# Convolution taps as three half-length filters, placed by the dense products; one norm chain for four query tiles

## The chip, the cores and the metric

The kernel runs on one core of a Trainium2 chip. The metric is device microseconds (us) of one execution, the median of three runs. The engines are named as in the profile: PE is TensorE's matmul row (PEld its weight loads), DVE is VectorE, ACT is ScalarE, POOL is GpSimd, SP is SyncE, which here issues the DMAs. Each engine works off its own instructions strictly in the order in which they were written down for it; engines meet only at semaphores.

## The reference

Two layers of an encoder trunk over 1024 positions of width 1024, all in float32. The change touches two things inside a layer: the convolution branch and the norms of the attention's queries.

```
h = rms_norm(x); z = h @ w_in[l]                     # 20 column tiles of 128
attention: q (4 tiles), k, v -> QK-norm, 2-D rotary embedding, softmax(q k^T / 8) v
hgrn2: 4 heads, forward and backward gated recurrence (two kernel passes of 2 heads)
conv: u = a * sigmoid(gate)                          # 256 channels, 1024 positions
      y[t] = sum over 31 taps of w[tap] * u[t + tap - 15]
      o_cv = silu(layer_norm(y + b))                 # mean and variance over the channels
x = x + concat(attention, hgrn2, conv) @ w_out[l]
x = x + relu(rms_norm(x) @ w1)^2 @ w2
```

## The kernel before

**Layout.** Everything is held transposed: 128 channels on the partitions, the 1024 positions along the free axis. The 256 convolution channels are two tiles (i = 0, 1). A *dense product* is one column tile of z: eight steps over the contraction (`dense_steps`, line 214), each of six 128x512 matmuls (a float32 product from high and low parts), 48 matmuls into one of two PSUM tiles named S (a ring of two). `evac` (line 321) lets DVE multiply the finished product by the row norm `Rb` into SBUF, and so frees the PSUM tile.

**Order of a layer's first part.** The column tiles come in the order of `ZORDER`: the four of the convolution (`conv_in`), then five of the first recurrence pass, `Hgrn(0).__init__` (lines 408 to 450: column 6 hq, 10 and 12 the two gates, 14 the output gate, 8 the values iv). The values are transposed on PE at the end of the constructor (line 447) and copied by ACT to `vt`. Then `h0.core()` (line 515) runs its steps interleaved with `qkv()` (columns 5 v, 4 k, 0 to 3 q) and with the convolution `cg = conv_all()`: the loop of lines 707 to 709 takes one step of `qg`, `cg`, `qg`, `cg` for each step of the core. After that come the five columns of `Hgrn(1)` (7, 11, 13, 15, 9), with the convolution's tail (`conv_tail`: mean, variance, normalization, silu) taken along in three steps, and then the attention.

**Convolution.** `conv(i)` (line 345) does on DVE one `tensor_scalar` for the middle tap and 30 `scalar_tensor_tensor` (line 357), each over nearly 1024 positions and each adding to the same y. `conv_tail` (line 371) needs both y: POOL adds them, PE sums over the channels (line 162, `tok_sums`, 128x1 results), ACT widens the sums (`widen`, line 168), PE transposes them back (`flip`, line 178), DVE subtracts; then squares, sums, `rstd` and flips again for the variance.

**Recurrence core.** For s = 1, 2, 4 ... 64 line 530 multiplies four slices of X by T, two on POOL and two on DVE, and then DVE's line 531 updates T. From s = 2 on, `scores` copies slices (ACT, line 487), multiplies them on PE (line 499) into banks of the ring e or c (two banks each), and DVE merges them into A (lines 506 and 510). Line 588 makes the output o.

**Norms of q and k.** PE sums squares (line 162); `rstd` (line 147) is a chain of 11 tiny DVE instructions. For k the result is widened and flipped (line 665 multiplies it in); for each of the four q tiles it runs on 16 columns and goes to `nqc`, which the attention's score pass (line 761) reads.

**What sets the order.** A scheduler writes down the order on each engine: it goes through the program in the order in which it is written, with a machine model of its own, and lets an engine take a later instruction when the next one isn't ready in that model. So the order on an engine is fixed before the run, and it needn't suit the real durations.

## Time and profile before

| | |
|---|---|
| median of three runs | 2541.44 us (2540.55 to 2541.88) |
| the profiled execution | 2538.31 us, its span 2536.5 us |
| PE busy | 2457.5 us (97%) |
| DVE busy | 1998.2 us (79%) |
| ACT, POOL busy | 1206.2 us, 734.1 us |
| granted clock of TensorE, mean over the span | 0.984 |

The profile is one execution. Its page gives the busy time of each engine, the chain of work that ended last, and groups of instructions by source line; the trace behind it is asked for stretches of time (windows), instructions in order (timeline), and waits. A granted clock of 1.00 is 2.4 GHz, of 0.50 it is 1.2 GHz. In the text *stretch A* is the time from the end of column 8's product to the recurrence's output o of the first pass (112 to 246 us in layer 0, 1374 to 1506 us in layer 1), *stretch B* the time from there to the start of column 9's product (246 to 302 us, 1506 to 1562 us).

### The profile page before, as it was taken

The numbers are of one execution on the slowest core, as the hardware profiler recorded it, in microseconds if no ns is written. First come the engines' busy times: TensorE is split into PE (matmuls) and PEld (weight loads), VectorE is DVE, ScalarE is ACT, GpSimd is POOL, SyncE is SP. The second block draws the span as 40 slices with busy tenths as digits, with TensorE's granted clock in tenths as the row PEclk, the third lists the DMA queues.
The fourth block names the chain that finished last, engine by engine and source line by source line (L and its number), as shares of the span: only waits on it lengthen the run. The fifth ranks groups of instructions, "written<-read, shape, count | busy, mean of one in ns | idle before, by whom it ended". The sixth has DMA issues, their size and how long they took to land.

```text
span 2536.5 us, 34033 instructions
## 1 busy us (share of the span) xinstructions
PE 2457.5 (97%) x12608; PEld 2024.9 (80%) x12608; DVE 1998.2 (79%) x3051; ACT 1206.2 (48%) x1960; POOL 734.1 (29%) x463
## 2 busy tenths in 40 slices
PE   8989999999999999999999999999999999999999
PEld 7767778878788887888887777888787888878887
DVE  6998599872887778987859985898638877789886
ACT  4222478863544443443433225787635444444332
POOL 0233566533034430000123325664330344200000
PEclk9998999999999999999999999999999999999999
DMA  4101310032244448554131113000322534574442
GB/s 160 57 25 63 104 34 18 14 116 105 75 170 163 141 159 322 160 174 156 67 108 51 42 63 104 17 18 26 133 89 87 173 137 163 187 279 158 161 152 91
DMA packets 113077, 286.99 MB, mean 113 GB/s; under 512 B 11408, under 2 KB 11664, under 8 KB 112912
## 3 DMA queue, kind: packets, MB, share of 16 engines
q1 hardware_dynamic: 112912, 284.83, 32.4%
q8 instruction: 99, 1.62, 0.3%
q14 instruction: 66, 0.54, 0.1%
HBM read 197.75 MB, written 87.03 MB: 112 GB/s over the span
## 4 chain that ended last, share of the span: by engine, by line
PE 79%; DVE 15%; ACT 3%; issue 2%; POOL 1%; DMA 1%; SPq 0%; DVEq 0%; ACTq 0%; POOLq 0%
PE S L223 15%; PE S L1201 10%; PE c L1000 10%; PE S L1000 7%; PE e L1000 7%; PE e L1201 6%; PE c L1201 6%; DVE x L357 4%; PE e L808 4%; PE c L787 4%; PE S L750 3%; PE e L499 2%; PE e L162 1%; PE e L588 1%; DVE wlo L200 1%
## 5 line engine op out<-in xcount | busy, mean ns | idle before, releaser
L223 PE MATMUL S<-xs,whi 128*128 128x512 f32 x1280 | 365.0, 407 | 8.8 <-ACT whi L199 7.4
L223 PEld LDWEIGHTS S<-xs,whi 128*128 128x128 f32 x1280 | 244.2, 194 | 65.0 <-ACT whi L199 7.4
L1201 PE MATMUL S<-xs,xs 128*128 128x512 f32 x816 | 201.6, 390 | 2.6 <-DVE xs L902 2.6
L223 PE MATMUL S<-xs,wlo 128*128 128x512 f32 x640 | 203.4, 399 | 0.0
L901 ACT ACTIVATE xs<-m 128x512 fp32r<-128x512 f32 x216 | 126.0, 619 | 141.6 <-DVE m L912 50.8
L766 POOL TENSOR_SCALAR P<-P,mx 128x1024 f32<-128x1024 f32 x124 | 142.4, 1148 | 164.2 <-DVE mx L765 129.8
L792 DVE TENSOR_TENSOR PT<-c,PT 128x512 fp32r<-128x512 f32 x256 | 171.2, 685 | 23.1 <-ACT PT L791 21.2
L1201 PEld LDWEIGHTS S<-xs,xs 128*128 128x128 f32 x816 | 152.9, 188 | 35.4 <-DVE xs L902 3.5
L791 ACT ACTIVATE PT<-c 128x512 fp32r<-128x512 f32 x256 | 147.7, 593 | 69.9 <-PE c L787 66.3
L199 ACT ACTIVATE whi<-raw 128x1024 fp32r<-128x1024 f32 x56 | 59.1, 1058 | 243.3 <-PE S L223 224.2
L808 PE MATMUL e<-PT,x 128*128 128x256 f32 x1024 | 173.8, 300 | 0.8 <-ACT PT L791 0.5
L761 DVE TENSOR_SCALAR_CACHE_REDUCE P<-S,nqc 128x1024 f32<-128x1024 f32 x124 | 158.6, 1279 | 15.7 <-PE S L750 8.0
L357 DVE SCALAR_TENSOR_TENSOR x<-x,par,x 128x1009 f32<-128x1009 f32 (+14 forms) x120 | 166.9, 1391 | 1.8
L787 PE MATMUL c<-cons,P 128*128 128x128 f32 x992 | 152.8, 278 | 10.5 <-POOL P L766 5.6
L902 DVE TENSOR_TENSOR xs<-m,xs 128x512 fp32r<-128x512 f32 x216 | 145.0, 695 | 22.0 <-ACT xs L901 22.0
L750 PE MATMUL S<-x,QS 128*128 128x512 f32 x480 | 153.9, 419 | 6.0 <-DVE P L761 5.7
L261 POOL TENSOR_TENSOR tmp<-tmp,tmp 128x1024 f32<-128x1024 f32 x19 | 50.6, 2664 | 360.1 <-ACT tmp L260 359.9
L764 ACT ACTIVATE P<-P,mx 128x1024 f32<-128x1024 f32 x124 | 142.5, 1149 | 25.3 <-DVE P L761 24.0
L808 PEld LDWEIGHTS e<-PT,x 128*128 128x128 f32 x1024 | 140.4, 195 | 8.4 <-ACT PT L791 2.0
L787 PEld LDWEIGHTS c<-cons,P 128*128 128x128 f32 x992 | 115.7, 141 | 36.4 <-issue 10.2
L223 PEld LDWEIGHTS S<-xs,wlo 128*128 128x128 f32 x640 | 123.3, 193 | 26.8 <-issue 0.3
L1201 PE MATMUL e<-xs,xs 128*128 128x512 f32 x552 | 140.8, 390 | 0.9 <-ACT xs L901 0.5
(310 smaller groups left out, 5639.0 us busy)
## 6 DMA issues: line engine op xcount, KB each, us to landing
m<-ad SPq DMA_DIRECT2D x104, 512.0 KB, 3.9
ad<-x SPq DMA_DIRECT2D x176, 256.0 KB, 2.2
raw<-w_in_t SPq DMA_DIRECT2D x40, 512.0 KB, 3.3
xs<-w_t SPq DMA_DIRECT2D x36, 512.0 KB, 3.9
raw<-w_t SPq DMA_DIRECT2D x36, 512.0 KB, 3.6
m<-w_t SPq DMA_DIRECT2D x32, 512.0 KB, 6.8
ad<-tmp SPq DMA_DIRECT2D x48, 256.0 KB, 2.3
x<-w_t SPq DMA_DIRECT2D x24, 512.0 KB, 4.8
```

The source lines that it names most:

```text
L223: nc.tensor.matmul(zp[h] if type(zp) is list else zp[:, h, :], w, xx[:, h * 512 : (h + 1) * 512], start=first, stop=last)
L357: nc.vector.scalar_tensor_tensor(y[:, lo:hi], u[:, lo + d : hi + d], par[:, l, wof + tap : wof + tap + 1], y[:, lo:hi], op0=ALU.mult, op1= ...
L750: nc.tensor.matmul(S[:, hb, :], qs, kk[:, hb * 512 : (hb + 1) * 512], start=first, stop=not first)
L761: nc.vector.tensor_scalar(Pt, S, nqc[:, j, ci : ci + 1], 3.0e38, op0=ALU.mult, op1=ALU.min, accum_out=mx[:, 1:2])
L764: nc.scalar.activation(Pt, Pt, AF.Exp, bias=mx[:, 1:2], scale=-1.0, accum_out=mx[:, 2:3])
L787: nc.tensor.transpose(t[:, q * P : (q + 1) * P], Pt[:, hb, q * P : (q + 1) * P], ident)
L791: nc.scalar.activation(hi, src, AF.Copy)
L792: nc.vector.tensor_tensor(lo, src, hi.bitcast(F32), op=ALU.subtract)
L808: nc.tensor.matmul(pvp[:, cs], VS[g][:, hb * 4 + kb, :], pt[:, kb, :], start=hb == 0 and n == 0, stop=hb == 1 and n == 7,)
L902: ordered("v", nc.vector.tensor_tensor(lo, src, hi.bitcast(F32), op=ALU.subtract))
L1000: nc.tensor.matmul(bank, w[i][:, kt * P : (kt + 1) * P], BC[name][kt][j], start=n == 0 and name not in ("M6", "M7", "M3"), stop=n == 11, s ...
L1201: nc.tensor.matmul(banks[dt], w[i][:, dt * P : (dt + 1) * P], a[j], start=n == 0 and name not in ("M6", "M7", "M3"), stop=n == 3 * SG - 1, ...
```

## The change

**Three half-length filters.** u is now written by POOL with its even positions in the first half of the tile and its odd ones in the second (a strided access). With E and O for even and odd taps, the even outputs are E(ue) + O(uo), and the odd ones are (E+O)(ue+uo) - E(ue) - O(uo), suitably shifted. So a convolution tile takes three filters over 512 positions: 15 taps on the even half, 16 on the odd half, 16 on the sum, with an extra column and a small edge correction; then three combining instructions, two of which write y interleaved. In place of 1 + 30 long instructions there are 3 + 44 half-length ones, one sum, three combinations and five tiny ones.

**Where the taps stand.** `behind` ties each `scalar_tensor_tensor` of a filter to the last matmul that `dense` has written down, for the scheduler's order alone: no semaphore comes of it. The constructors now take convolution steps along with their products (`pace`: after which of the eight contraction steps), from the first column on; the loop over `h0.core()` takes fewer. Two steps of the generator are written as one `cg` step. The loop that finished both convolutions before the attention's keys is gone.

**The tail has two more stages**: a stop after each widening.

**Moved.** The transposes of iv go from the constructor into the core (`turned`, after its first step). v's second part is done after contraction step 6 of column 4, not 2.

**Query norms.** Each q tile writes its mean square into `nqc`; one `rstd` chain over 64 columns for all four follows after `qkv` (`query_norms`).

```diff
-    def rstd(src, n, scale):
+    def rstd(src, n, scale, work=None):
...
+    def behind(i):
+        tc.add_manual_dep(i.ins, pe_last[0].ins.name, mybir.DependencyInfo(
+            mybir.DependencyClass.NoSync, mybir.DependencyReason.DATA), reason="order")
...
-        def ztile(col):
+        def ztile(col, pace=()):
             got = []
-            drain(zsteps(col, got.append))
+            for k, _ in enumerate(zsteps(col, got.append)):
+                for _ in range(pace.count(k)):
+                    next(cg, None)
             return got[0]
...
+        def fir(dst, src, taps, shift=0):
+            n, m = dst.shape[1], src.shape[1]
+            for k, (d, w) in enumerate(sorted(taps, key=lambda t: abs(t[0] + shift))):
+                d += shift
+                lo, hi = max(0, -d), min(n, m - d)
+                if k == 0:
+                    nc.vector.tensor_scalar(dst, src[:, d : d + n], w, 0.0, op0=ALU.mult, op1=ALU.add)
+                else:
+                    behind(nc.vector.scalar_tensor_tensor(
+                        dst[:, lo:hi], src[:, lo + d : hi + d], w, dst[:, lo:hi], op0=ALU.mult, op1=ALU.add
+                    ))
+                yield
+
+        def conv_steps(i):
...
+            nc.vector.tensor_tensor(s[:, 1:H], uo[:, 0 : H - 1], ue[:, 1:H], op=ALU.add)
+            yield
+            second = fir(even, ue, [(d, tap(2 * d)) for d in range(-7, 8)])
+            for _ in fir(odd, uo, [(d, tap(2 * d + 1)) for d in range(-8, 8)]):
+                yield
+                if next(second, 1) is None:
+                    yield
+            yield from fir(uo, s, [(d, hs[:, d + 8 : d + 9]) for d in range(-8, 8)], 1)
...
         def conv(i):
-            u = us[i]
...
+            for k, _ in enumerate(conv_steps(i)):
+                if k % 2:
+                    yield
...
-                evac(ztile(8 + ls), iv)
+                evac(ztile(8 + ls, (1, 4) if ls else ()), iv)
+
+            def turned(self):
...
+                self.turned()
...
+        def query_norms():
+            y = rstd(nqc.rearrange("p a b -> p (a b)"), 64, 1.0 / 64, tmp())
...
-                    if k == 2 and rest:
+                    if rest and k == (6 if col == 4 else 2):
...
-        for _ in h0.core():
-            for g in (qg, cg, qg, cg):
-                next(g, None)
+        for n, _ in enumerate(h0.core()):
+            next(qg, None)
+            if n > 3 and n % 4 < 3:
+                next(cg, None)
+            next(qg, None)
         drain(qg)
-        while not ys[1:]:
-            next(cg)
+        query_norms()
```

**Place 1: DVE around the evacuation of column 8 (iv), layer 0.** Before, L327 is `evac`, L357 a tap, L200 the low part of a weight tile; S2_122 is column 8's product.

```order
L327 TENSOR_TENSOR tmp_112_651<-S2_116_658,Rb_76_307 128x1024
L200 TENSOR_TENSOR wlo_121_717<-raw_119_714,whi_120_716 128x1024
L357 SCALAR_TENSOR_TENSOR x8_135_807<-x8_79_341,par_13_76,x8_135_807 128x1017
...
L357 SCALAR_TENSOR_TENSOR x8_135_807<-x8_79_341,par_13_76,x8_135_807 128x1012
L327 TENSOR_TENSOR m4_118_713<-S2_122_720,Rb_76_307 128x1024
L458 TENSOR_TENSOR m4_130_791<-X_93_465 128x512 x2
```

In the changed kernel the same work has the lines L338 (`evac`), L367 (a half-length tap) and L203, and S2_126 is column 8's product:

```order
L367 SCALAR_TENSOR_TENSOR x8_79_341<-x8_102_489,nwa_103_490,x8_79_341 128x511
L367 SCALAR_TENSOR_TENSOR x8_79_341<-x8_102_489,nwa_103_490,x8_79_341 128x509
L338 TENSOR_TENSOR tmp_116_691<-S2_120_698,Rb_76_307 128x1024
L203 TENSOR_TENSOR wlo_125_765<-raw_123_762,whi_124_764 128x1024
L338 TENSOR_TENSOR m4_122_761<-S2_126_768,Rb_76_307 128x1024
L511 TENSOR_TENSOR m4_132_827<-X_93_465 128x512 x2
```

Six taps that stood between the weight tile and the evacuation of iv are gone from there; four half-length ones stand ahead of the evacuation of column 14 (S2_120).

**Place 2: PE at the transposes of iv, layer 0.** Before (S2_134 is the next product, column 5; L447 the transposes):

```order
L223 MATMUL S2_122_720<-xs_50_145,wlo_109_591 128x512 x2
L223 MATMUL S2_134_800<-xs_33_103,whi_114_654 128x512 x2
L223 MATMUL S2_134_800<-xs_34_104,whi_114_654 128x512 x2
L223 MATMUL S2_134_800<-xs_33_103,wlo_115_655 128x512 x2
L223 MATMUL S2_134_800<-xs_35_108,whi_114_654 128x512
L447 MATMUL e_123_770<-cons_14_77,m4_118_713 128x128 x4
```

and now (S2_136 is column 5, L500 the transposes):

```order
L232 MATMUL S2_126_768<-xs_50_145,wlo_113_621 128x512 x2
L232 MATMUL S2_136_836<-xs_33_103,whi_118_694 128x512 x2
L232 MATMUL S2_136_836<-xs_34_104,whi_118_694 128x512 x2
L232 MATMUL S2_136_836<-xs_33_103,wlo_119_695 128x512 x2
L232 MATMUL S2_136_836<-xs_35_108,whi_118_694 128x512 x2
L232 MATMUL S2_136_836<-xs_36_109,whi_118_694 128x512 x2
L232 MATMUL S2_136_836<-xs_35_108,wlo_119_695 128x512 x2
L500 MATMUL e_137_849<-cons_14_77,m4_122_761 128x128 x4
```

Twelve matmuls of column 5 now stand ahead of the transposes, where there were seven.

**Place 3: PE between the convolution's variance sums and the flips of its result, layer 0** (layer 1 has the same order). Before (L162 the sums, L178 the flips, S2_310 column 15's product; the rows left out are 12 more matmuls of it, 19 in all):

```order
L162 MATMUL e_296_2026<-cons_14_77,tmp_289_1959 128x1 x8
L223 MATMUL S2_310_2089<-xs_33_103,whi_281_1878 128x512 x2
L223 MATMUL S2_310_2089<-xs_34_104,whi_281_1878 128x512 x2
L223 MATMUL S2_310_2089<-xs_33_103,wlo_282_1879 128x512 x2
...
L223 MATMUL S2_310_2089<-xs_42_124,whi_281_1878 128x512
L178 MATMUL e_301_2051<-cons_14_77,tmp_300_2049 128x128 x4
L178 MATMUL e_302_2058<-cons_14_77,tmp_300_2049 128x128 x4
```

and now (L165 the sums, L181 the flips, L809 the attention's first two score products, S2_288 column 15 and S2_310 column 9):

```order
L232 MATMUL S2_288_2033<-xs_50_145,wlo_272_1875 128x512 x2
L809 MATMUL S2_300_2134<-x8_259_1795,x8_257_1787 128x512
L165 MATMUL e_293_2095<-cons_14_77,tmp_291_2066 128x1 x8
L809 MATMUL S2_300_2134<-x8_259_1795,x8_257_1787 128x512
L809 MATMUL S2_300_2134<-x8_260_1796,x8_257_1787 128x512 x2
L181 MATMUL e_311_2176<-cons_14_77,tmp_297_2118 128x128 x3
L809 MATMUL S2_303_2145<-x8_259_1795,x8_257_1787 128x512 x2
L809 MATMUL S2_303_2145<-x8_260_1796,x8_257_1787 128x512 x2
L181 MATMUL e_311_2176<-cons_14_77,tmp_297_2118 128x128
L181 MATMUL e_312_2183<-cons_14_77,tmp_297_2118 128x128 x4
L232 MATMUL S2_310_2163<-xs_33_103,whi_276_1949 128x512 x2
```

Three score matmuls now stand between the sums and the flips, where there were 19 of a dense product, and column 9's product starts behind the flips.

**How many.** By the same orders, DVE has between the evacuation of iv and o (stretch A) 31 long taps, one long first tap and 50 tiny norm instructions before, and now 33 half-length taps, two half-length first taps, four half-length sums and combinations and 14 tiny norm instructions. Ahead of it there were 27 long taps, now 34 half-length ones and three first taps; behind it there were two long taps and one q tile's norm chain, now 21 half-length taps, one first tap, three combinations and the chain over 64 columns. Layer 1 has one long tap less in A before and the same now. On ACT, the table for the sigmoid of the convolution's tail is now loaded between the second and the third exponential of the attention, and the one for the exponential again behind it; before, the tail's sigmoids stood ahead of the first exponential.

## Rows read from the trace of the kernel before

**Rows 1.** Windows of the whole core: stretch, its length, busy time of PE, PEld, DVE, ACT and POOL with the number of instructions, granted clock, DMA share and GB/s. The rows are, for layer 0 and then for layer 1, the products ahead of stretch A, stretch A and stretch B.

```profile
59.00:112.00 53.00, 53.00 (x235) 43.92 (x234) 51.00 (x39) 14.86 (x15) 11.35 (x4) 1.00 0.21 73
112.00:246.00 134.00, 119.02 (x759) 93.48 (x758) 125.87 (x188) 35.55 (x51) 44.61 (x20) 0.91 0.13 45
246.00:302.00 56.00, 53.91 (x272) 44.68 (x271) 36.38 (x66) 22.79 (x23) 21.50 (x9) 0.97 0.22 75
...
1374.00:1506.00 132.00, 119.84 (x764) 94.14 (x762) 126.29 (x187) 35.39 (x51) 42.39 (x20) 0.92 0.13 46
1506.00:1562.00 56.00, 53.92 (x269) 44.62 (x269) 34.44 (x66) 23.23 (x23) 22.17 (x9) 0.97 0.23 77
```

**Rows 2.** The chain of work that ended last, inside 112 to 250 us: shares by engine and line.

```profile
by line: PE S L223 14.7%; DVE x L357 14.7%; issue 9.5%; DVE A L510 6.7%; DVE X L530 6.7%; PE e L162 5.4%; PE e L588 5.2%; DVE wlo L200 5.0%; DVE T L531 4.4%; POOL X L530 3.3%; DVE tmp L629 3.2%; PE e L499 3.1%; DVE nwt L154 2.0%; DVE A L506
```

**Rows 3.** Timeline of PE: start, us, line, operation, tiles, count, and in brackets PE's idle time ahead of it and who ended it. Layer 0's waits in stretch A, one of stretch B, then layer 1's two largest.

```profile
116.92 1.97 PE L447 MATMUL e<-cons,m 128*128 128x128 f32 x8 [4.25 <-DVE m L327]
145.50 1.97 PE L642 MATMUL e<-cons,tmp 128*128 128x128 f32 x8 [5.70 <-DVE A L506]
179.66 1.10 PE L178 MATMUL e<-cons,tmp 128*128 128x128 f32 x8 [1.20 <-ACT tmp L168]
189.64 2.67 PE L499 MATMUL e<-m,m 64*128 64x128 f32 x16 [2.02 <-DVE tmp L665]
...
219.61 1.15 PE L544 MATMUL c<-cons,X 128*128 128x128 f32 x8 [1.46 <-ACT T L545]
...
265.66 1.09 PE L178 MATMUL e<-cons,tmp 128*128 128x128 f32 x8 [1.67 <-ACT tmp L168]
...
1379.03 1.97 PE L447 MATMUL e<-cons,m 128*128 128x128 f32 x8 [4.26 <-DVE m L327]
1405.09 1.97 PE L642 MATMUL e<-cons,tmp 128*128 128x128 f32 x8 [2.77 <-DVE A L506]
```

**Rows 4.** Windows of 5 us, columns as in rows 1: behind PE's wait for iv, behind the wait of 2.02 us, and behind the wait of 1.67 us in stretch B.

```profile
115.00:120.00 5.00, 3.08 (x12) 2.79 (x13) 5.00 (x5) 1.19 (x2) 2.45 (x2) 0.50 0.02 3
...
190.00:195.00 5.00, 5.00 (x23) 4.20 (x22) 5.00 (x7) 2.65 (x5) 3.50 (x2) 0.50 0.55 189
...
265.00:270.00 5.00, 4.34 (x23) 3.74 (x24) 2.51 (x3) 1.67 (x2) 0.00 (x0) 1.00 0.36 126
```

**Rows 5.** Timeline of DVE, columns as in rows 3: seven taps in a row, the six ahead of iv's evacuation, that evacuation, a pair of 128x512 merges, a tap beside POOL's rotary product, and from stretch B the steps of the variance's chain (first and last) and the products with the flips.

```profile
69.88 9.14 DVE L357 SCALAR_TENSOR_TENSOR x<-x,par,x 128x1012 f32<-128x1012 f32 x7
105.15 10.58 DVE L357 SCALAR_TENSOR_TENSOR x<-x,par,x 128x1017 f32<-128x1017 f32 x6
115.65 1.22 DVE L327 TENSOR_TENSOR m<-S,Rb 128x1024 f32<-128x1024 f32 x1
...
152.39 1.35 DVE L510 COPY_PREDICATED A<-masks,c 128x512 f32<-128x512 uint8 x2
...
167.88 0.17 DVE L152 TENSOR_SCALAR nwy<-nwa 128x16 int32<-128x16 int32 x1
168.00 1.28 DVE L357 SCALAR_TENSOR_TENSOR x<-x,par,x 128x1016 f32<-128x1016 f32 x1
169.19 0.17 DVE L154 SCALAR_TENSOR_TENSOR nwt<-nwy 128x16 f32<-128x16 f32 x1
...
183.21 3.45 DVE L357 SCALAR_TENSOR_TENSOR x<-x,par,x 128x1023 f32<-128x1023 f32 x1
...
287.36 0.17 DVE L151 TENSOR_SCALAR nwa<-e 128x8 f32<-128x8 f32 x1 [0.45 <-PE e L162]
...
290.42 0.17 DVE L156 SCALAR_TENSOR_TENSOR nwy<-nwt,nwy 128x8 f32<-128x8 f32 x1
292.49 2.48 DVE L399 TENSOR_TENSOR x<-x,e 128x512 f32<-128x512 f32 x4 [1.91 <-PE e L178]
```

**Rows 6.** DVE's groups by line with shapes kept apart, over the whole span: names, shapes, count, busy time in us, mean ns, idle time ahead of them.

```profile
L1013 DVE SCALAR_TENSOR_TENSOR tmp<-tmp,Rb 128x512 f32<-128x512 f32 x64 | 54.1, 866 | 1.3 <-ACT Rb L237 0.9
...
L1013 DVE SCALAR_TENSOR_TENSOR x<-x,Rb 128x512 f32<-128x512 f32 x64 | 42.5, 685 | 0.1
...
L349 DVE TENSOR_SCALAR x<-x,par 128x1024 f32<-128x1024 f32 x4 | 5.3, 1328 | 0.0
```

**Rows 7.** DVE's groups in stretch A of layer 0, columns as in rows 6.

```profile
L357 DVE SCALAR_TENSOR_TENSOR x<-x,par,x 128x1014 f32<-128x1014 f32 (+14 forms) x34 | 45.5, 1340 | 0.2
```

**Rows 8.** Timeline of POOL, columns as in rows 3: the product that makes u, the recurrence's products for s = 4 behind DVE's T, and the rotary product beside the tap of rows 5.

```profile
47.28 2.40 POOL L342 TENSOR_TENSOR x<-tmp,tmp 128x1024 f32<-128x1024 f32 x1 [46.84 <-ACT tmp L340]
...
133.93 4.61 POOL L530 TENSOR_TENSOR X<-X,T 128x512 f32<-128x512 f32 x2 [1.14 <-DVE T L531]
...
181.11 4.47 POOL L627 TENSOR_TENSOR tmp<-tmp,x 128x1024 f32<-128x1024 f32 x1 [16.98 <-DVE tmp L626]
```

**Rows 9.** Timeline of PE in stretch B: the variance sums, the next four matmuls of column 15, and the flips.

```profile
285.49 1.84 PE L162 MATMUL e<-cons,tmp 128*128 128x1 f32 x16
287.19 1.19 PE L223 MATMUL S<-xs,whi 128*128 128x512 f32 x4
...
291.73 1.09 PE L178 MATMUL e<-cons,tmp 128*128 128x128 f32 x8
```

**Rows 10.** Timeline of ACT there: the widening of the variance's result, and the table load ahead of the first exponential.

```profile
290.62 1.06 ACT L168 ACTIVATE tmp<-nwy 128x1024 f32<-128x1024 f32 x1 [1.66 <-DVE nwy L156]
...
301.96 1.28 ACT L436 ACT_TABLE_LOAD   x1
```

More of the change, by code (lines that the diff above doesn't have):

```diff
@@ L145, in lower_bounds @@
         nc.vector.tensor_scalar(oml, lbt, -1.0, 1.0, op0=ALU.mult, op1=ALU.add)
-    def rstd(src, n, scale):
-        a = cst.t([P, 16], "nwa", bufs=2)[:, :n]
-        y = cst.t([P, 16], "nwy", bufs=3)[:, :n]
-        t = cst.t([P, 16], "nwt", bufs=2)[:, :n]
+    def rstd(src, n, scale, work=None):
+        if work is None:
+            a = cst.t([P, 16], "nwa", bufs=2)[:, :n]
+            y = cst.t([P, 16], "nwy", bufs=3)[:, :n]
+            t = cst.t([P, 16], "nwt", bufs=2)[:, :n]
+        else:
+            a, y, t = (work[:, i * n : (i + 1) * n] for i in range(3))
         nc.vector.tensor_scalar(a, src, scale, EPS, op0=ALU.mult, op1=ALU.add)
@@ L341, in conv_in @@
             u = x8()
-            nc.gpsimd.tensor_tensor(u, a, s, op=ALU.mult)
+            nc.gpsimd.tensor_tensor(
+                u.rearrange("p (h n) -> p n h", h=2), a.rearrange("p (n h) -> p n h", h=2),
+                s.rearrange("p (n h) -> p n h", h=2), op=ALU.mult,
+            )
             us.append(u)
-        def conv(i):
-            u = us[i]
-            y = x8()
-            wof = PAR["cw"][0] + i * CK
-            nc.vector.tensor_scalar(
-                y, u, par[:, l, wof + CPAD : wof + CPAD + 1], pv(l, "cb", i), op0=ALU.mult, op1=ALU.add
-            )
-            for tap in range(CK):
-                d = tap - CPAD
-                if d == 0:
-                    continue
-                lo, hi = max(0, -d), min(L, L - d)
-                nc.vector.scalar_tensor_tensor(
-                    y[:, lo:hi], u[:, lo + d : hi + d], par[:, l, wof + tap : wof + tap + 1], y[:, lo:hi],
-                    op0=ALU.mult, op1=ALU.add,
-                )
-                yield
-            ys.append(y)
+        def fir(dst, src, taps, shift=0):
[5 more added lines that the diff above has]
+                    nc.vector.tensor_scalar(dst, src[:, d : d + n], w, 0.0, op0=ALU.mult, op1=ALU.add)
+                else:
+                    behind(nc.vector.scalar_tensor_tensor(
+                        dst[:, lo:hi], src[:, lo + d : hi + d], w, dst[:, lo:hi], op0=ALU.mult, op1=ALU.add
+                    ))
+                yield
@@ L429, in __init__ @@
                 gl = tmp()
-                evac(ztile(14 + ls), gl)
-                if ls == 1:
-                    next(cg, None)
+                evac(ztile(14 + ls, (2, 6) if ls else full[:4]), gl)
                 gate = tmp()
@@ L690, in qpart @@
             nc.sync.dma_start(qd[j], qz)
+        def query_norms():
+            y = rstd(nqc.rearrange("p a b -> p (a b)"), 64, 1.0 / 64, tmp())
+            for j in range(4):
+                nc.vector.scalar_tensor_tensor(
+                    nqc[:, j].rearrange("p (a b) -> p a b", b=2),
+                    y[:, 16 * j : 16 * j + 16].rearrange("p (a b) -> p a b", b=2), -0.125,
+                    rc.unsqueeze(2).to_broadcast([P, 8, 2]), op0=ALU.mult, op1=ALU.mult,
+                )
         def qkv():
```

56 lines of the change are left out of this document (41 added, 15 removed).

## The prediction

> **What bounds the kernel now.** I read the windows first [rows 1], then the chain inside the one that stands out [rows 2], then PE's and DVE's timelines there. Ahead of stretch A PE is busy 53.0 of 53.0 us, so nothing that DVE saves there can be won. In stretch A of layer 0 PE works 119.0 of 134.0 us and DVE 125.9, and the clock row is 0.91. PE's loss is therefore 15.0 us of idle time and, at the lower of its two levels (1.2 GHz) for part of the time, about 0.09 x 134 x (119/134) = 10.7 us of slow work: 25.7 us together. In layer 1 it is 132.0 - 119.8 = 12.2 and 0.08 x 132 x 0.91 = 9.6, 21.8 us. DVE idles only 8.1 and 5.7 us there. In stretch B the picture is turned round: PE 53.9 of 56.0, DVE 36.4. So stretch A is paced by both engines, with DVE the fuller one; B is paced by PE.
>
> The chain agrees [rows 2]: DVE's taps (L357) hold 14.7% of it, as much as the dense products (L223), beside the recurrence's steps on DVE and POOL (L510, L530, L531) and 9.5% of issue. The waits are the visible part [rows 3]: PE stands 4.25 us for iv, because iv's evacuation starts at 115.65 behind six taps that took 10.58 us [rows 5]; 5.70 us (layer 1: 2.77) for a merge into A; and 1.20, 2.02 and 1.46 us elsewhere. Behind a wait the clock may be down: 0.50, that is 1.2 GHz, in the 5 us behind the waits of 4.25 and 2.02, but 1.00 behind that of 1.67 [rows 4].
>
> **The taps' price.** Seven long taps take 9.14 us, 1.31 each [rows 5]; the mean in A, with those beside POOL, is 1.34 [rows 7]. A tap alone starts 1.19 before the next instruction (168.00 to 169.19), and a tiny one 0.12 (167.88 to 168.00) [rows 5]. No half tap is in the trace. Its neighbours are L1013 at 128x512: 685 ns for one form, 866 for the other [rows 6]; and two merges of 128x512 that take 1.35 together, 0.62 to 0.73 each [rows 5]. I take 0.65, since the 685 ns is a duration and the next instruction starts a little earlier, as it does with the long ones; 0.62 and 0.87 are the ends. A half-length first tap is half of 1328 ns [rows 6], 0.66.
>
> **Stretch A, DVE.** By the orders, before: 31 x 1.19 + 1.33 + 50 x 0.12 = 44.2 us. Now: 33 x 0.65 + 2 x 0.66 + 4 x 0.62 + 14 x 0.12 = 27.0. DVE is relieved of 17 us (10 if a half tap costs 0.87). That is the ceiling of what A can win as long as DVE paces it: 134 to 117.
>
> **Stretch A, PE.** The 4.25 for iv goes: place 1 shows its evacuation right behind the weight tile, and place 2 gives PE five more matmuls to cover it. The 5.70 goes or shrinks, as DVE is earlier. Left are 1.20 + 2.02 + 1.46 = 4.7 us [rows 3], whose releasers are ACT and a norm chain, not taps. New waits come in their place, because the recurrence's chain (T on DVE, then POOL's 4.61 us for s = 4 and its like [rows 8], then T again) doesn't get shorter than its own steps: nothing to two waits like layer 1's 2.77, I take 4. The clock drops once or twice more, 3 us. So 11.7 of PE's loss remain, and it gains 14.0 in layer 0 and 10.1 in layer 1. Two engines that pace a stretch by turns give somewhat less than the lower view: **12 and 10 us taken**.
>
> **Stretch B.** DVE gets 21 x 0.65 + 0.66 + 3 x 0.62 + a chain of 64 columns (15 tiny ones, 2 us) = 18, and loses two taps and a q chain, 2 x 1.19 + 13 x 0.12 = 4: 14 us more into the 19.6 that it has free [rows 1]. That fits, with little over. The cost is place 3. From the end of the variance sums (285.49 + 1.84 = 287.33) to the flips (291.73) pass 4.4 us [rows 9]: a chain of eleven dependent tiny steps on DVE (287.36 to 290.59 [rows 5]), then 1.06 us of ACT's widening [rows 10]. Before, a dense product's 19 matmuls covered it. Now three score matmuls do, at four in 1.19 [rows 9] some 0.9 us, and all of column 9 is queued behind the flips on PE. That is a new wait of 3.5 us per layer. Behind waits of 2.02 and 4.25 us the clock was at 0.50, and 3.08 us of work at that level cost 1.5 more [rows 4]. So **5 us lost per layer**. The lower end is 1.8: no clock loss, and the old wait of 1.67 at the first flips gone [rows 3]. The upper end is 8: the evacuation of column 15 (1.22 [rows 5]) late behind the same chain, and twice the clock loss.
>
> The Trainium skill, "TensorE: Matmul & The Clock Gate", section "HAM oscillation — how this bites in real kernels", has it that a PE which pauses for its inputs again and again starts again cold each time, at 1.2 GHz. The rows agree at two of the three waits, not at that of 1.67 us. By the rule both layers pay, as in the sum here; by the 1.67 row alone it would be 3.5 per layer and a median of 2526.
>
> **At nothing.** POOL's strided u: 2.40 us before [rows 8]; 4.6 if a stride doubles it, as two 128x512 with strides take 4.61 [rows 8]. Its first taps stand ahead of A, where PE is never idle; if that cover were gone, it would cost 2 us once per tile. Two more table loads on ACT per layer, 1.28 each [rows 10], run beside column 9's product of 48 matmuls, about 11 us; uncovered 2.6. The taps moved ahead of A fill a DVE that has 2 us free in 53 [rows 1], but 27 x 1.19 = 32 us go there and 34 x 0.65 + 3 x 0.66 = 24 come. `behind` makes no semaphore.
>
> **The sum.** Layer 0: 12 - 5 = 7; layer 1: 10 - 5 = 5. The profiled execution of 2538.3 becomes 2526.3. The median of the runs is 3.1 above the profiled time, so **2529 us**.
>
> **Rivals.**
> 1. *DVE drops out of A altogether and PE paces it.* Then only the 4 us of new waits per layer remain of 25.7 + 21.8: 47.5 - 8 - 10 (B) = 29.5, giving 2512. For it: 17 us of relief exceed PE's 15.0 of idle time, and clock loss follows idle time. Against: the chain names POOL (L530, 3.3%) and tiny steps, which keep their length.
> 2. *The recurrence's chain paces A, and DVE's relief is only idle time.* DVE waits for POOL and PE where it now does taps. Only iv's wait goes, 4.25 and 2.3 of clock, 13 us in two layers; B takes 10. Gain 3, **2538**, no measurable change. For it: L510, L530 (on DVE and POOL), L531 and issue hold 30% of the chain. Against: DVE idles 8.1 us in A, so a chain without taps on it would show holes there.
> 3. *Slower: B becomes DVE's.* If half taps cost 0.87 there, DVE needs 36.4 + 14 + 21 x 0.22 = 55 of 56 us, and each of the tail's four crossings (sums and flips of the mean, sums and flips of the variance) stands behind taps, with PE in order behind it. Four crossings of 4.4 are 17.6 per layer against 12 and 10 won: 13 us slower, **2554**. It decides once B loses over 11 us per layer. For it: 21 half taps stand there where two long ones stood, and place 3 has no dense work. Against: the spare 5.6 us, and that the tail's crossings come after the last taps.
>
> **How the numbers follow.** Forecast (a gain of 6 to 20 us, median 2521 to 2535) 0.60; rival 1 (2505 to 2520) 0.13; rival 2 (2535 to 2543) 0.14; rival 3 (from 2543 up) 0.13. A measurement can tell about 0.2%, 5 us, from no change. Faster: 0.59 of the forecast, all of rival 1 and 0.03 of rival 2, together 0.75. Within: 0.01, 0.10 of rival 2 and 0.02 of rival 3, 0.13. Slower: 0.12. The range of 2511 to 2543 takes in the forecast, most of rival 2 and half of rival 1; about 0.2 is left out, below and above.
>
> **What the profile after would show.** No wait at iv's transposes (was 4.25); half taps 0.65 apart; DVE's total 20 to 30 us lower; stretch A 10 to 14 us shorter with PE's idle time near 9; a new wait of about 3.5 at the flips behind the variance chain, and the clock below 1 behind it; two more table loads per layer that nobody waits for. Wrong, if half taps take 0.8 or more, if A stays within 4 us of 134 with DVE idle (rival 2), or if PE waits at more than one of the tail's crossings (rival 3).

## The result, and the profile after

The changed kernel takes **2550.39 us** (median of eight runs, 2545.58 to 2556.82) against 2541.26 us (2536.51 to 2545.55) of the kernel before beside it: a ratio of 1.0038 [1.0026, 1.0049]. It is slower, by 9 us; 2529 was forecast, with a range up to 2543. The profiled execution took 2548.46 us, its span 2546.3 us at a mean granted clock of 0.984, so 9.8 us more span than before at the same clock. Of the twelve runs of the experiment e1 below two were slow, the profiled one (2740.82 us) among them, so its stages are left out there; its median without the two is 2536.60 us.

First the page: busy time of each engine.

```profile
PE 2473.0 (97%) x12608; PEld 2023.3 (79%) x12608; DVE 1959.8 (77%) x3081; ACT 1210.1 (48%) x1980; POOL 705.3 (28%) x463
```

DVE does 38.4 us less, and PE is busy 15.5 us more, at the same mean clock and with the same number of matmuls. Next, where it went. The table is worked out from the starts and ends of matmuls in the two traces (us, layer 0 / layer 1). The stretches join one another: A, from the end of column 8's product to the last matmul of o; from there to the end of column 15; the *gap* from there to the start of column 9; the *attention's beginning*, from there to the last value product (the stretch holds column 9 and the whole attention, but what differs arises at its beginning: layer 0's value products lie up to 8.5 us later than before within its first 65 us, and 4.7 at its end); and the rest of the layer, in which the w_out projection and w1's product lie (w1's first matmul starts 0.2 us before w_out's last ends, and the two overlap by that much).

| | A | o to col. 15's end | gap | attention's beginning | w_out | w1 |
|---|---|---|---|---|---|---|
| before | 134.8 / 132.2 | 53.6 / 53.6 | 2.5 / 2.5 | 265.1 / 265.0 | 82.2 / 82.2 | 316.3 / 316.3 |
| after | 117.1 / 118.8 | 57.1 / 55.5 | 10.2 / 10.2 | 269.8 / 268.8 | 84.2 / 84.2 | 320.2 / 320.6 |
| difference | -17.7 / -13.4 | +3.5 / +1.9 | +7.7 / +7.7 | +4.7 / +3.8 | +2.0 / +2.0 | +3.9 / +4.3 |

A gained more than forecast (12 and 10), B lost more (11.2 and 9.6 where 5 was taken). Part of both is one and the same: before, 17 matmuls of column 7 stood ahead of the end of o, and now they all stand behind it (counted in the traces: A holds 304 and 287 matmuls of the dense products, B 175 and 192). At 226.7 ns each that is 3.9 us, which A hands on to B in each layer. Without it A gains 13.8 and 9.5 and B loses 7.3 and 5.7. Together, from column 8's end to column 9's start, they give -6.5 and -3.9, near to the forecast's -7 and -5. What makes the kernel slower stands in the last three columns, and none of them was in the sum. The windows show the products ahead of A, A, B, B's part up to the end of column 15, the gap with column 9's product, and the first score passes; then A and B of layer 1 (columns as in [rows 1]):

```profile
59.00:111.00 52.00, 52.00 (x231) 43.07 (x230) 41.88 (x51) 14.50 (x14) 8.82 (x4) 1.00 0.23 81
111.00:228.00 117.00, 111.09 (x746) 86.60 (x745) 104.00 (x160) 34.61 (x55) 36.68 (x20) 0.99 0.13 46
228.00:295.00 67.00, 61.40 (x288) 50.40 (x287) 46.10 (x90) 23.53 (x24) 18.27 (x8) 0.90 0.23 75
228.00:285.00 57.00, 54.61 (x256) 44.95 (x255) 41.24 (x75) 18.80 (x19) 14.11 (x6) 0.94 0.24 79
285.00:306.00 21.00, 17.79 (x81) 14.57 (x81) 8.06 (x22) 10.12 (x13) 15.06 (x10) 0.84 0.19 66
306.00:345.00 39.00, 30.37 (x163) 24.13 (x161) 37.02 (x59) 28.99 (x49) 28.05 (x19) 0.84 0.23 74
1377.00:1496.00 119.00, 113.02 (x748) 88.00 (x746) 104.36 (x160) 35.04 (x55) 36.78 (x20) 0.97 0.12 45
1496.00:1561.50 65.50, 59.92 (x288) 49.36 (x287) 46.04 (x90) 23.52 (x24) 18.19 (x8) 0.92 0.24 77
```

In A of layer 0 DVE went from 125.9 us to 104.0 [rows 1], PE's idle time from 15.0 to 5.9 and the clock from 0.91 to 0.99. From 306 us on, where the attention begins, PE idles 8.6 of 39 us. PE's timeline has the waits (columns as in [rows 3]); A's four, the tail's three with the work between them, and two of the attention:

```profile
119.97 1.96 PE L530 MATMUL e<-m,cons 128*128 128x512 f32 x4 [1.01 <-DVE tmp L523]
144.79 1.13 PE L553 MATMUL e<-m,m 64*128 64x128 f32 x8 [1.66 <-DVE x L701]
162.82 1.09 PE L181 MATMUL e<-cons,tmp 128*128 128x128 f32 x8 [0.92 <-ACT tmp L171]
170.48 1.73 PE L553 MATMUL e<-m,m 64*128 64x128 f32 x16 [2.30 <-DVE tmp L719]
...
268.64 1.95 PE L165 MATMUL e<-cons,tmp 128*128 128x1 f32 x16 [2.19 <-POOL tmp L425]
...
286.36 1.95 PE L165 MATMUL e<-cons,tmp 128*128 128x1 f32 x16 [1.33 <-POOL tmp L443]
288.17 1.61 PE L809 MATMUL S<-x,x 128*128 128x512 f32 x3
291.66 0.90 PE L181 MATMUL e<-cons,tmp 128*128 128x128 f32 x3 [1.88 <-ACT tmp L171]
292.21 2.05 PE L809 MATMUL S<-x,x 128*128 128x512 f32 x4
294.07 1.18 PE L181 MATMUL e<-cons,tmp 128*128 128x128 f32 x5
294.99 1.18 PE L232 MATMUL S<-xs,whi 128*128 128x512 f32 x4
...
315.27 0.58 PE L867 MATMUL e<-PT,x 128*128 128x256 f32 x1 [4.76 <-ACT PT L850]
...
342.12 0.66 PE L846 MATMUL c<-cons,P 128*128 128x128 f32 x4 [2.04 <-POOL P L825]
```

The waits of 4.25 and 5.70 us [rows 3] are gone. The gap is the stretch from the end of column 15 (284.81) to column 9 (294.99): two waits, of 1.33 and 1.88, the tail's sums and flips, and score products that run there slowly (three in 1.61 us, where four matmuls of the same 128x512 shape took 1.19 in [rows 9]).

### The profile page after: what moved, and what is told of

It reads as the page before. It is cut to its first block, busy times and chain, and to the rows that moved or that the text cites. A ratio compares the mean times of both kernels' runs of the same rounds, so it can differ in the third digit from the quotient of the medians.

```text
span 2546.3 us, 34081 instructions
## 1 busy us (share of the span) xinstructions
PE 2473.0 (97%) x12608; PEld 2023.3 (79%) x12608; DVE 1959.8 (77%) x3081; ACT 1210.1 (48%) x1980; POOL 705.3 (28%) x463
## 5 line engine op out<-in xcount | busy, mean ns | idle before, releaser
L867 PE MATMUL e<-PT,x 128*128 128x256 f32 x1024 | 169.3, 300 | 11.1 <-ACT PT L850 10.8
L809 PE MATMUL S<-x,QS 128*128 128x512 f32 x480 | 151.5, 422 | 3.8 <-DVE P L820 2.0
L867 PEld LDWEIGHTS e<-PT,x 128*128 128x128 f32 x1024 | 137.8, 195 | 17.5 <-ACT PT L850 13.1
L1260 PE MATMUL c<-xs,xs 128*128 128x512 f32 x552 | 139.3, 389 | 0.0
```

The lines of the kernel that those rows point to most:

```text
L809: nc.tensor.matmul(S[:, hb, :], qs, kk[:, hb * 512 : (hb + 1) * 512], start=first, stop=not first)
L867: nc.tensor.matmul(pvp[:, cs], VS[g][:, hb * 4 + kb, :], pt[:, kb, :], start=hb == 0 and n == 0, stop=hb == 1 and n == 7,)
L1260: nc.tensor.matmul(banks[dt], w[i][:, dt * P : (dt + 1) * P], a[j], start=n == 0 and name not in ("M6", "M7", "M3"), stop=n == 3 * SG - 1, ...
```

## The experiments

Three questions: what slows the projections, which no edit touches (theory P: a tile's place in memory); what delays the attention (K: the keys come late behind the tail's transfers on SP's queue; T: the gap, with the tail's crossings bare); and which part of the change gains in A (F: the half-length form, or the places). e1 is the changed kernel with one unused tile more; "e1 with" means that kernel plus the edit named. All results in one table; stages as above, with w_out and w1 added up, from the one profiled execution of each. Since o's end moves against the column tiles from kernel to kernel, the time from column 8's end to column 9's start stands beside A. Ratios are against the kernel before on the same chip.

| | median us | ratio [95%] | A | col. 8 to col. 9 | gap | attention's beginning | w_out + w1 |
|---|---|---|---|---|---|---|---|
| before | 2541.26 | | 134.8 / 132.2 | 190.9 / 188.3 | 2.5 / 2.5 | 265.1 / 265.0 | 398.4 / 398.4 |
| after | 2550.39 | 1.0038 [1.0026, 1.0049] | 117.1 / 118.8 | 184.4 / 184.4 | 10.2 / 10.2 | 269.8 / 268.8 | 404.2 / 404.7 |
| e1 | 2537.09 | 0.9984 [0.9976, 0.9993] | | | | | |
| e2 | 2552.20 | 1.0049 [1.0037, 1.0061] | 134.6 / 135.6 | 190.7 / 192.8 | 2.5 / 2.5 | 265.0 / 265.0 | 403.5 / 403.8 |
| e3 | 2542.72 | 1.0010 [1.0001, 1.0018] | 121.4 / 125.0 | 183.9 / 186.3 | 2.6 / 3.1 | 270.9 / 272.4 | 397.3 / 397.7 |
| e4 | 2535.33 | 0.9979 [0.9970, 0.9987] | 121.5 / 120.0 | 184.6 / 183.1 | 10.5 / 10.5 | 270.4 / 269.9 | 397.3 / 397.6 |
| e5 | 2524.36 | 0.9943 [0.9926, 0.9959] | 117.1 / 117.0 | 184.9 / 184.3 | 10.8 / 10.2 | 264.5 / 263.4 | 397.8 / 397.4 |
| e6 | 2543.36 | 1.0017 [1.0007, 1.0026] | 121.9 / 124.8 | 186.9 / 190.0 | 8.5 / 8.5 | 271.5 / 269.9 | 397.3 / 397.8 |
| e7 | 2546.44 | 1.0024 [1.0012, 1.0036] | 156.1 / 154.0 | 198.3 / 193.4 | 2.5 / 2.5 | 263.7 / 263.5 | 398.6 / 398.3 |
| e8 | 2534.67 | 0.9984 [0.9969, 0.9999] | 117.6 / 117.6 | 183.4 / 185.6 | 9.4 / 9.9 | 270.4 / 268.1 | 397.7 / 397.9 |
| e9 | 2549.75 | 1.0033 [1.0020, 1.0045] | 120.1 / 123.4 | 178.2 / 183.0 | 2.5 / 2.5 | 280.9 / 280.9 | 397.3 / 397.4 |
| e10 | 2539.6 (one run) | | 117.1 / 118.9 | 184.4 / 186.1 | 10.2 / 10.2 | 270.2 / 270.5 | 397.4 / 397.4 |
| e11 | 2540.76 (one run) | | 117.1 / 116.2 | 184.4 / 183.8 | 10.2 / 10.5 | 270.4 / 268.7 | 401.6 / 400.5 |
| e12 | 2542.96 | 1.0007 [0.9998, 1.0016] | 118.5 / 121.6 | 186.6 / 187.3 | 11.0 / 10.2 | 270.0 / 269.6 | 398.3 / 397.6 |
| e13 | 2549.51 | 1.0030 [1.0020, 1.0040] | 125.2 / 124.1 | 190.9 / 189.3 | 9.4 / 9.4 | 269.7 / 269.4 | 397.7 / 397.8 |

### P: the projections

The matmuls of w1 have the same shapes, order and clock in both kernels. PE's timeline, one group of twelve with each half of the weights. Before:

```profile
763.94 2.88 PE L1000 MATMUL e<-m,whi 128*128 128x512 f32 x12
766.66 2.88 PE L1000 MATMUL c<-m,wlo 128*128 128x512 f32 x12
```

and after:

```profile
764.43 2.95 PE L1059 MATMUL e<-m,whi 128*128 128x512 f32 x12
767.22 2.96 PE L1059 MATMUL c<-m,wlo 128*128 128x512 f32 x12
```

From start to start that is 2.72 and 2.79 us, 226.7 and 232.5 ns for one matmul, with no wait, and PE never idle there. The change dropped the tile `ms` (two buffers of 64 bytes on each partition) from the pool of constants. By the program, the pools of constants, weights and `xs` are laid out from the left end of SBUF, one behind the other, so the weights now lie 128 bytes lower; the streamed tiles `m` are in a pool laid out from the right end, and did not move.

**e1**: the tile back, unused.

```diff
+        cst.t([P, 16], "ms", bufs=2)
```

> The changed kernel with one tile more, which nothing reads or writes (two buffers of 64 bytes, where the mean squares of a q tile stood before). Theory P (the place of the tiles): without that tile every tile on the left side of SBUF has moved by 128 bytes against those on the right, and matmuls that stream from the right (the tiles m and mx) start every 229 to 238 ns in place of 227. Then the output projection goes back from 84 to 82 us and the product with w1 from 320 to 316 us in each layer, and the median falls by 12 us, from 2550 to 2538. Rival: these stages are longer for another reason (transfers or other engines that come at other times); then both stay as they are and the median stays at 2550.

Measured: 2537.09. The 128 bytes that nobody reads are worth 13 us.

**e2**: the kernel before without the tile; the mean squares go straight to `nqc`.

```diff
-            ms = cst.t([P, 8, 2], "ms", bufs=2)
-            nc.vector.tensor_tensor(ms, spv, r2b, op=ALU.mult)
-            y = rstd(ms.rearrange("p a b -> p (a b)"), 16, 1.0 / 64)
+            nc.vector.tensor_tensor(nqc[:, j].rearrange("p (a b) -> p a b", b=2), spv, r2b, op=ALU.mult)
+            y = rstd(nqc[:, j], 16, 1.0 / 64)
```

> The kernel before without that tile: the mean squares of a q tile are written straight into nqc. Theory P: the same 12 us appear with nothing else changed, in the output projection (82 to 84 us) and the product with w1 (316 to 320 us): 2541 becomes 2553. Rival: within 2 us of 2541.

Measured: 2552.20, 11 more. The profiled execution is 13.4 us longer in its span, and 10.5 us of that lie in w_out and w1 (403.5 + 403.8 against 398.4 + 398.4). Of the rest, 3.4 in A of layer 1 is not explained.

**e10** and **e11**: the changed kernel, with 128 bytes spent on the *other* side, and with half of the tile back.

```diff
+    rpad = Pool("rpad", side="right")
+    rpad.t([P, 32], "rpad")
```

```diff
+        cst.t([P, 16], "ms")
```

> The changed kernel with a spare 128 bytes on the right side of SBUF: now the tiles of both sides lie 128 bytes lower than in the kernel before, and the distance between the weights (left) and what streams from the right is as it was there. If the distance matters: output projection 82 us, product with w1 316 us, 2538 in all. If the address itself matters (of either side): 84 and 320, 2550.

> The changed kernel with 64 of the 128 bytes given back, so that the left side lies 64 bytes off. If any offset costs the same: 84 and 320 us in these stages. If the loss goes with the offset: 83 and 318. If 64 bytes are no offset: 82 and 316.

PE's timeline of e10, then of e11, at the same place:

```profile
761.01 2.88 PE L1061 MATMUL e<-m,whi 128*128 128x512 f32 x12
763.73 2.88 PE L1061 MATMUL c<-m,wlo 128*128 128x512 f32 x12
```

```profile
763.75 2.93 PE L1060 MATMUL e<-m,whi 128*128 128x512 f32 x12
766.51 2.91 PE L1060 MATMUL c<-m,wlo 128*128 128x512 f32 x12
```

With both sides moved by 128 bytes the price is back at 226.7 ns, with 64 bytes it is between. So it isn't the weights' address alone that counts but its distance from the streamed tile (the right side was not moved alone). P holds.

### K and T: the attention's beginning, and the gap

SP's queue of the changed kernel shows both halves of kd's load and the tail's stores between them; then POOL's last products of the tail, and ACT's and DVE's instructions that make the keys:

```profile
298.57 0.45 SPq L777 DMA_DIRECT2D tmp<-kd  x1
305.10 2.68 SPq L459 DMA_DIRECT2D mixd<-tmp  x2
307.83 0.45 SPq L778 DMA_DIRECT2D tmp<-kd  x1
```

```profile
302.68 4.75 POOL L458 TENSOR_TENSOR tmp<-tmp,x 128x1024 f32<-128x1024 f32 x2
```

```profile
311.83 1.06 ACT L208 ACTIVATE x<-tmp 128x1024 fp32r<-128x1024 f32 x1 [0.67 <-DMA tmp<-kd]
```

```profile
312.98 2.36 DVE L209 TENSOR_TENSOR x<-tmp,x 128x1024 fp32r<-128x1024 f32 x1
```

The stores of `mixd` wait for the tail's last products on POOL, and the load behind them waits too, though nothing holds it but its place in the queue. The kernel before had the stores ahead of that load as well, and its keys begin at the same time:

```profile
301.35 5.05 SPq L405 DMA_DIRECT2D mixd<-tmp  x2
306.91 0.45 SPq L718 DMA_DIRECT2D tmp<-kd  x1
```

```profile
311.80 1.06 ACT L205 ACTIVATE x<-tmp 128x1024 fp32r<-128x1024 f32 x1 [6.07 <-DMA tmp<-kd]
```

So the changed kernel comes to column 9 some 7 us earlier (294.99 against 302), and then waits for keys that come when they always came.

**e5**: e1 with the tail's stores issued behind the loads of the keys.

```diff
-                nc.sync.dma_start(mixd[2 + i], s)
+                late.append((2 + i, s))
...
+        for i, s in late:
+            nc.sync.dma_start(mixd[i], s)
```

> As e1, but the two writes of the convolution's result to DRAM are written behind the loading of the second keys, so that the second half of these keys no longer stands behind them on SP's queue (307.8 us in layer 0, the first half 298.6). Theory K (the attention's beginning hangs on these keys, and they on the convolution's tail): both halves are issued near 299 us and land near 304 in place of 312; of the 5.2 and 3.8 us lost in the attention's beginning most come back: 2537 becomes 2529 to 2532. Rival A (ACT's two extra table loads and late sigmoids cost it): no change, 2537.

Measured: **2524.36**, 13 us below e1 by the medians (10 by the two ratios), and 0.9943 [0.9926, 0.9959] of the kernel before, 16 us below its 2540.18 on the same chip: the best kernel of the study. SP's queue and DVE:

```profile
298.67 0.45 SPq L778 DMA_DIRECT2D tmp<-kd  x1
299.18 0.66 SPq L779 DMA_DIRECT2D tmp<-kd  x1
305.21 2.69 SPq L840 DMA_DIRECT2D mixd<-tmp  x2
```

```profile
309.64 1.83 DVE L209 TENSOR_TENSOR x<-tmp,x 128x1024 fp32r<-128x1024 f32 x1
```

The second half is issued 8.7 us earlier and the keys are 3.3 us earlier. The attention's beginning is 264.5 / 263.4, as before the change or less. K holds: against the changed kernel's 269.8 / 268.8 that is 10.7 us, and against e10's 270.2 / 270.5, the changed kernel with the projections' price taken away the other way, 12.8, as much as e5 gains on e1. Two things did not come as expected: the keys are 3.3 us earlier and not 8, and the gain is larger than the 5 to 8 us forecast. The extra table loads on ACT, rival A's cause, are still there in e5's trace, so they are not what delayed the attention.

**e3** tests T: e1 with the convolution further on at column 9 (a step in each of the core's turns, 25 in place of 19, and fewer in the columns behind it).

```diff
-            if n > 3 and n % 4 < 3:
+            if n > 3:
...
-                    evac(ztile(10 + 2 * d + ls, full[:5] if ls == 0 else full if d == 0 else (2, 6)), zt)
+                    evac(ztile(10 + 2 * d + ls, full[:5] if ls == 0 else (1, 5) if d else (3,)), zt)
...
-                evac(ztile(8 + ls, (1, 4) if ls else ()), iv)
+                evac(ztile(8 + ls, () if ls else ()), iv)
```

> As e1, and the loop over the core takes 25 convolution steps in place of 19, the products behind it fewer, so that the tail's sums and flips stand inside dense products again. Theory T (the tail is late, because 21 half taps stand behind the recurrence): the gap ahead of column 9's product falls from 10.2 to about 2.5 us, the attention's beginning loses nothing, and DVE has room for 12 more half taps in the recurrence (8 us into 13 idle): some 14 and 10 us won per layer against the kernel before, 2517. Rival: the attention's beginning waits for its keys or for ACT in any case; then 5 and 4 us are lost there again and the median is 2526 or more.

Measured: 2542.72, 26 above what T expected and 6 above e1. The gap closes, but A is 121.4 / 125.0 and the attention's beginning takes 5.8 and 7.4 us more than before. DVE's timeline in front of column 9's evacuation:

```profile
310.07 1.22 DVE L209 TENSOR_TENSOR x<-tmp,x 128x1024 fp32r<-128x1024 f32 x1 [10.97 <-ACT x L208]
```

DVE stands 10.97 us for the keys, and the evacuation stands behind it. T's gap is there, but what it saved went into the wait for the keys, and A is longer, with 114.6 us of DVE's work in it in layer 0 where the changed kernel has 104.0.

**e6**: e3 with the tail's last two products, and a gate product of the second pass, on DVE in place of POOL, so that POOL hands on sooner.

> As e3, but the convolution's last products and the product with the second pass's output gate run on DVE, not on POOL, where they take 2.4 us each in a queue. Theory K: in e3 the keys' buffer comes free behind POOL's queue, which now ends some 6 us earlier; DVE's wait of 11 us for the keys shrinks to 5 or less and the 6.5 and 8 us lost in the attention's beginning to 3 or less: 2543 becomes 2533. Rival A: the beginning is set by ACT and the clock, and DVE has 3.6 us more to do: 2543 to 2548.

Measured: 2543.36, no better. The keys are earlier, but the two products take 4.60 us on DVE and PE waits for the score pass queued behind them (DVE's timeline, then PE's):

```profile
291.94 4.60 DVE L458 TENSOR_TENSOR tmp<-tmp,x 128x1024 f32<-128x1024 f32 x2 [0.78 <-ACT tmp L457]
```

```profile
297.80 2.08 PE L232 MATMUL S<-xs,whi 128*128 128x512 f32 x4 [5.38 <-DVE x L821]
```

**e9**: e5 with the variance's sums and flips tied behind matmuls of the dense products, and the tail's steps moved to fit (steps 2 and 5 of column 13, 1 of 15, 0 and 5 of 9).

```diff
-            tok_sums(sp, sq[0], mean_w)
+            tok_sums(sp, sq[0], mean_w, tie=True)
...
-                b = flip(w, h)
+                b = flip(w, h, tie=True)
```

> As e5, with the variance's sums and flips tied behind the first and the sixth contraction step of column 9's product, so that this product covers DVE's chain and ACT's widening. If the gap ahead of column 9 (10.8 us in e5, 2.5 in the kernel before) is the wait behind that chain, it falls to 3 us or less in both layers and column 9 ends some 8 us earlier; 2524 becomes 2508 to 2514. Rival: the tail's end moves back as much, and the attention's beginning gives the 8 us back as it did before e5: 2520 to 2526.

Measured: 2549.75, 25 worse than e5 and outside both expectations. The gap falls to 2.5 as wanted; the attention's beginning grows by 16.4 / 17.5. PE's timeline:

```profile
318.59 1.94 PE L853 MATMUL c<-cons,m 128*128 128x128 f32 x8 [12.47 <-DVE mx L829]
```

The tail now ends inside the attention's beginning, where its products stand among the second recurrence pass's on POOL and DVE. Hidden in one place, it is late in the next.

### F: the form, or the places

**e4**: e1 with the old 31 long taps over an unstrided u, in the same places (25 steps for each tile).

```diff
-            for k, _ in enumerate(conv_steps(i)):
-                if k % 2:
+            for tap in range(CK):
...
+                behind(nc.vector.scalar_tensor_tensor(
+                    y[:, lo:hi], u[:, lo + d : hi + d], par[:, l, wof + tap : wof + tap + 1], y[:, lo:hi],
+                    op0=ALU.mult, op1=ALU.add,
+                ))
+                n += 1
+                if n * 25 // 31 > (n - 1) * 25 // 31 and n < 31:
```

> As e1, but with the 31 full-length taps of before (u in its old order), in the places and steps of the changed kernel. Theory F (places win, not the form): a tile's filter costs DVE 36.5 us in place of 33.5, so the recurrence is at most 4 us longer per layer than in e1 and still 10 us shorter than before; 2538 + 4 to 8 = 2542 to 2546. Rival (the half-length filters free DVE): the recurrence goes back to 134 and 132 us, the rest stays, and the median is above 2560.

Measured: 2535.33, as good as e1 with its half-length filters, and better than F expected. A keeps all but 4.4 and 1.2 us of its gain. The window of e4's A:

```profile
111.30:232.90 121.60, 114.81 (x746) 89.13 (x745) 106.36 (x140) 35.38 (x52) 38.27 (x20) 0.96 0.15 50
```

DVE is relieved of 19.5 of its 125.9 us [rows 1] with taps as long as before; 22 of them stand between column 8's end and the end of o, where 34 stood.

**e7**: the reverse, the kernel before with the three half-length filters and the strided u alone, in the old places and without ties.

> The kernel before with the three half-length filters and the rearranged u alone: old steps in the loop, no ties to PE, old tail, old norms, old transposes. Theory F (places win, not the form): PE's wait for iv stays (3 to 5 us), the recurrence is 0 to 4 us shorter per layer, 2536 to 2541. Rival (the form frees DVE): the recurrence falls below 124 us, 2528 or less.

Measured: 2546.44, slower than before. (Its A isn't to be compared, since part of the later columns ran ahead of o; from column 8's end to column 9's start it takes 198.3 and 193.4 us against 190.9 and 188.3.) The old waits stay, and one at the tail's sums is new; PE's timeline:

```profile
115.74 1.09 PE L488 MATMUL e<-cons,m 128*128 128x128 f32 x8 [3.63 <-DVE m L327]
...
141.03 1.97 PE L683 MATMUL e<-cons,tmp 128*128 128x128 f32 x8 [2.96 <-DVE A L547]
...
238.31 2.08 PE L162 MATMUL e<-cons,tmp 128*128 128x1 f32 x16 [3.09 <-POOL tmp L414]
```

**e8**: e1 with a norm chain for each q tile, as before. **e12**: e1 with iv's transposes in the constructor again (`self.turned()` moved there).

> As e1, with the norms of the four query tiles as separate chains of 16 columns again. The 36 tiny instructions that come back into the recurrence are 4 us of DVE there, which has 13 idle in 117: if idle time covers them, the recurrence stays within 1 us and the median at 2537. Rival (their steps hold up what the recurrence waits for): 3 to 5 us longer per layer, 2543 to 2547.

> As e1, with the transposes of iv in the constructor again. If the taps' new places alone won the recurrence's time, iv's evacuation comes 1.3 us after the product's end and PE waits some 2 us there (0 in e1): the recurrence 1 to 3 us longer per layer, 2538 to 2542. Rival (moving the transposes won it): the recurrence goes back by 5 us or more per layer, 2547 or more.

Measured: 2534.67, so the shared chain gains nothing that can be told; and 2542.96, so the moved transposes are worth about 6 us, just above the range given for the places alone and below the rival's, and A shows 1.4 and 2.8 of it against the changed kernel.

**e13**: e4 with e8's and e12's edits: long taps, a norm chain for each tile, transposes as before. Left are the places, the ties and the tail's stops.

> As e4 (full-length taps, 31 per tile, the tile of 128 bytes kept), with the norms of each q tile as before and the transposes of iv in the constructor: of the change only the new places of the taps, their ties to PE and the tail's two stops are left. If places alone win the recurrence's time: it is still 9 to 13 us shorter per layer than in the kernel before, and the median is 2533 to 2542. Rival (form, norms and transposes each hide a part that shows once all three are gone): the recurrence is at most 5 us shorter, and the median above 2548.

Measured: 2549.51, 9 us slower than the kernel before: the median is the rival's. A is 9.6 and 8.1 us shorter than before, which looks like the theory's side, but 11 matmuls of column 7 (2.5 us) have left it, and from column 8's end to column 9's start nothing is won: 190.9 and 189.3 against 190.9 and 188.3. So the places alone do not carry the gain. With long taps in the new places, the shared chain and the moved transposes together are worth 14 us (e4 against e13); taken singly from e1, with half-length taps, they are worth nothing and 6. The parts don't add up, and half-length taps without these two were not tried in the new places.

## Why the prediction was wrong

The forecast was missed by 21 us. Of these, 12.1 lie in w_out and w1, 8.5 in the attention's beginning and 1.6 in A and B; the three add up to a little more than the miss.

**Taps: right.** A half tap took 0.66 us from start to start, 0.65 was taken (DVE's timeline):

```profile
249.41 0.74 DVE L367 SCALAR_TENSOR_TENSOR x<-x,nwa,x 128x510 f32<-128x510 f32 x1
250.07 0.22 DVE L157 SCALAR_TENSOR_TENSOR tmp<-tmp 128x64 f32<-128x64 f32 x1
```

DVE's total fell by 38.4 us, not by 20 to 30.

**Stretch A: the mechanism and nearly the size right.** 12 and 10 us were taken; 17.7 and 13.4 were measured, 13.8 and 9.5 of them without the matmuls that went to B. DVE was relieved of 21.9 us (17 reckoned). Of PE's loss 11.7 us were to remain; by the windows 5.9 us of idle time and about 1.1 of clock (0.01 x 111) remain in layer 0, 6.0 and 3.4 in layer 1. The two new waits that I took at 4 are 1.01 and 1.66, and the 5.70 is gone. What the prediction did not separate is *why* DVE is relieved: e4 shows that fewer long taps in A do it nearly as well as half-length ones (19.5 us), and e7 that shorter ones in the old places win nothing.

**Stretch B: a term that was mis-sized.** I took 5 per layer, with 8 as the upper end; 11.2 and 9.6 were measured, 7.3 and 5.7 without the matmuls that came from A. Rival 3's sign, waits at more than one of the tail's crossings, came, but not its cause: PE's waits have POOL's products (2.19, 1.33) and ACT's widening (1.88) as their releasers, and DVE had room, 41.2 of 57 us and 8.1 of 21. I priced one crossing of the tail, the variance's flips, and left out the sums ahead of it and those of the mean, which stand bare as well. That the idle time grew by the 3.5 us taken (2.1 to 5.6 in layer 0's B) is luck: it came as three waits, not as one. Too small was the clock's part, 1.5 us: by the rows of B it is 0.10 x 61.4 - 0.03 x 53.9 = 4.5 us in layer 0 and 3.2 in layer 1, an estimate from rounded rows. The clock fell behind the waits and the narrow sums that follow them, to 0.84 between 285 and 306 us and to 0.75 in this window:

```profile
290.00:300.00 10.00, 8.34 (x34) 7.02 (x35) 6.68 (x14) 7.26 (x9) 5.45 (x4) 0.75 0.24 92
```

The Trainium skill, "TensorE: Matmul & The Clock Gate", section "HAM oscillation — how this bites in real kernels", describes a PE that starts cold again after each wait for its inputs. The trace agrees as far as these rows go: the wait of 1.33 us ends at 286.36, and the three score products from 288.17 on take 1.61 us.

A and B together are nearly as forecast, -10.4 against -12. With these alone the kernel would have come to about 2531.

**"At nothing": the step that failed.** The sum passes on to the kernel's end what A and B win, as if nothing behind column 9 waited for anything else. I looked at the instructions that moved (tables, taps, the strided product) and not at the queue that the tail's stores stand in. Column 9 starts 7 us earlier in layer 0, but the keys are made when they were (311.80 and 311.83), since the second half of their load stands behind these stores. That costs 8.5 us in the attention's beginning of the changed kernel; e5 removes it.

**A term that was missing.** The removal of the tile `ms` stood in the change, had no place in the sum, and cost 12.1 us in w_out and w1 (13 by e1's median). Nothing in the profile of before shows it. No rival covered it either.

With these two mended the same change takes 2524 us (e5), 5 below the forecast: its mechanism, DVE's relief in A, is real. Whether e5's later stores would help the kernel before as well was not tried.

**Open.** Why A is longer in e3 and e6 than in the changed kernel, beyond DVE's extra work there, and why the attention's beginning gains nothing in e3, beyond the wait shown. Which of the places, the shared chain and the transposes are needed together for the gain is open; ties and places were not parted, nor were the tail's stops tried alone, nor e3's edit together with e5's.

## What to carry to other kernels

A change's price is not only in the instructions that it moves: look for each in-order queue, a DMA queue as much as an engine's, at what stands behind the moved instruction and doesn't depend on it. When an untouched product gets slower by a few per cent with no wait and at the same clock, look at where its tiles lie before looking for a cause in the schedule; an unused tile of the size of the one removed is a test of one line. When a stretch gets shorter, count what work has left it: here 3.9 us of a stretch's gain were matmuls that had only gone to the next one. And try the parts of a change separately and without each other: here the shorter form alone made the kernel slower (e7), the new places alone did too (e13), and the gain was there with long taps as well (e4).

## What the runs showed of the hardware

A 128x512 matmul whose weights lie on the left and whose streamed tile on the right took 226.7 ns from start to start at one distance between them, and 226.7 again when both had moved by 128 bytes. With the weights 64 bytes lower, and so 64 bytes more between them, the group shown took 230 ns, with 128 bytes more 232.5. On average over w1's matmuls that stream `m`, worked out from the starts in the traces, it is 227.7 before, 230.3 in e11 and 234.2 in the changed kernel (most of them between 229 and 238). Those that stream `xs`, which lies on the weights' side and moves with them, took 227.2 before and 227.6 in the changed kernel. Over the kernel this is 12 us, 0.5%. What in the chip makes the distance count, and at which other distances, was not tried.

On SP's queue a load that nothing else held was issued 9.3 us after its first half, behind two stores that waited for POOL, and 0.5 us after it when the stores stood behind (e5).
